# Strassen's products for gate and up in 12 pairs of column tiles, with adaLN columns by VectorE in the opening

## The chip, the cores and the metric

The kernel runs on one core of one Trainium2 chip. The metric is the device time of one execution in microseconds (us), taken as the median of several runs; lower is better. Engines are named as the profile names them: PE (TensorE), DVE (VectorE), ACT (ScalarE), POOL (GpSimd) and SP (SyncE, which issues most loads).

## The reference

One layer of a streaming encoder on 512 tokens of width 1024, all in float32. Each sub-layer gets shift, scale and gate from a conditioning vector c ("adaLN"):

```python
mod = (silu(c) @ w_ada + b_ada)            # 9 x 1024 numbers
h = rms_norm(x, g_pre) * (1 + scale) + shift
h = (silu(h @ w_gate) * (h @ w_up)) @ w_down     # FFN, D_FF = 2816
x = x + 0.5 * (1 + gate) * rms_norm(h, g_post)
... # mixer: spatial gating group and attention with forgetting, one projection in, one out
... # a second FFN like the first, with weights and adaLN numbers of its own
```

## The kernel before

All activations lie transposed: features on partitions (eight k-tiles of 128), the 512 tokens on the free axis. The order on every engine is written out by the program: code order is issue order (`manual_schedule`), and generators registered with `beside` put in their steps when `tick(us)` says that so many us of matmuls have gone by.

Precision comes from splitting. Each float32 operand is a high part (a cast by ACT) and a low part (float32 minus high, by DVE), and `mm3` makes each product of three matmuls, high x high, high x low, low x high. Weights are split on the chip: `Pair.hi` (L193) casts, `Pair.lo` (L203) subtracts; for some weights of the mixer `lo` runs as an ACT negation and an accumulating DMA from POOL's queue (L200, L201).

An FFN has 22 column tiles f of 128 gate and 128 up columns. `gate_up` runs 48 matmuls of 512 tokens for a tile (2 x 8 k-tiles x 3), `activate` turns the two results into the hidden tile h[f]: silu by ACT (L474), times up by DVE (L475), cast by ACT (L476), low part by DVE (L479). GROUPS splits the 22 tiles into 7, 7 and 8. After each group the eight output tiles m get the group's share (`pd`), copied into y by ACT for the first group (L542) and added by DVE for the others (L544). The last group does this in two halves of 256 tokens, so that the closing norm of one half runs beside the downs of the other. In the second FFN, the first four tiles also run in halves, since x arrives in halves.

Loads come through a queue of expected sources (`expect`, `load_next`) into the pool rp, two buffers of 1 MB. adaLN's columns are sums along rows of w_ada times silu(c): `mod_column` (L297) is one DVE instruction with an accumulated output. In the opening, a list of steps written by hand (START), the columns for k-tiles 0 and 1 are instead made by PE (BY_PE, matmuls into ps_mod, L306); the six others by DVE. The normalised x tile (xt, L647; high part of xm by ACT, L649; low part by DVE, L651) of a k-tile can be made when its columns are there, and the matmuls of the first three column tiles go k-tile by k-tile behind it. silu(c) as a row on all partitions (`crow`) is a broadcast DMA followed by an ACT silu. The other seven sets of columns come between the groups' steps (`between`).

Of the kernel before, what the change touches and what calls it, by code (L numbers as in the profile page):

```python
# [17 lines left out]
P = 128  # L18
D = 1024
# [6 lines left out]
GROUPS = (range(0, 7), range(7, 14), range(14, 22))  # L26
# [8 lines left out]
    1.3, 0, 0.9, 0.9, 0.7, 0.9, 0.8, 0, 0, 1.7, 1.9, 0, 0, 0.7, 1.4, 0.2, 1.6, 1, 0.5, 0.2, 0.6,  # L35
    0.7, 0, 1.1, 0.4, 0.4, 0, 0, 0.4, 1.6, 0.4, 0.7, 0.4, 1, 0.7,
# [3 lines left out]
    1.2, 1.4, 1.7, 1.7, 0, 9, 0.4, 0.4, 0, 0.7, 1.3, 0.7, 1.2, 0.7, 0.7, 0.7,  # L40
# [20 lines left out]
def pace(name, usual):  # L61
# [4 lines left out]
BY_PE = (0, 1)  # L66

# [22 lines left out]
def kernel(ctx: ExitStack, tc: tile.TileContext, a: dict, out: bass.AP):  # L90
# [81 lines left out]
    def expect(src, width):  # L172
        loads.append((src, width))
# [3 lines left out]
    def load_next(parts=1):  # L177
        if loads:
            src, width = loads.pop(0)
            raw = rp.tile([P, 2 * WSLOT], F32, tag="raw", name="raw")  # L180
            for i in range(parts):
                c = slice(i * width // parts, (i + 1) * width // parts)
                nc.sync.dma_start(raw[:, c], src[:, c])
            arrived.append(raw)

    class Pair:
        def __init__(self, n):
            self.n, self.raw, self.u, self.done = n, arrived.pop(0), [None, None], 0

        def hi(self, j, alloc=None):  # L190
            w = [P, 2, WSLOT] if alloc is None else [P, 2, D]
            self.u[j] = (alloc or wtile)(w, F32R, "wu")
            nc.scalar.copy(self.u[j][:, 0, : self.n], self.raw[:, j * self.n : (j + 1) * self.n])  # L193


        def lo(self, j, how="vector"):
            u, n = self.u[j], self.n
            raw, hi = self.raw[:, j * n : (j + 1) * n], u[:, 0, :n].bitcast(F32)
            if how == "transfer":
                nc.scalar.activation(u[:, 1, :n], hi, AF.Copy, scale=-1.0)  # L200
                nc.gpsimd.dma_start(u[:, 1, :n], raw, accum_op=ALU.add)  # L201
            else:
                (nc.vector if how == "vector" else nc.gpsimd).tensor_sub(u[:, 1, :n], raw, hi)  # L203
            self.done += 1
            if self.done == 2:
                load_next()
# [8 lines left out]
    def mm3(ps, lh, ll, rh, rl, start, stop):  # L215
        nc.tensor.matmul(ps, lhsT=lh, rhs=rh, start=start, stop=False)  # L216
        nc.tensor.matmul(ps, lhsT=lh, rhs=rl, start=False, stop=False)  # L217
        nc.tensor.matmul(ps, lhsT=ll, rhs=rh, start=False, stop=stop)  # L218
        return 3 * ps.shape[-1] * MM
# [75 lines left out]

    def mod_column(j, kt, raw):
        nc.vector.scalar_tensor_tensor(raw, raw, 1.0, crow, op0=ALU.mult, op1=ALU.mult,  # L297
                                       accum_out=msum[:, j * KT + kt : j * KT + kt + 1])

    def mod_first(kt, raws):  # L300
        both = lambda c: c[:, : 2 * KT].rearrange("p (j k) -> p j k", j=2)[:, :, kt]
        if kt in BY_PE:
            ps = psax("ps_mod")
            for j in range(2):
                for k in range(KT):
                    nc.tensor.matmul(ps[:, j : j + 1], lhsT=raws[j][:, k], rhs=sc[:, k : k + 1], start=j + k == 0, stop=j == 1 and k == KT - 1)  # L306
            src = ps[:, :2]
        else:
            for j in range(2):
                mod_column(j, kt, raws[j])  # L310
            src = both(msum)
# [1057 lines left out]
```

## Time and profile before

| what | value |
|---|---|
| median of 3 runs | 1037.07 us (1035.49 to 1040.47) |
| the profiled execution | 1040.04 us, of which the span 1038.2 |
| mean granted clock of PE | 0.974 |
| PE busy | 992.6 us, 5246 matmuls |
| DVE busy | 543.5 us, 1032 instructions |
| ACT busy | 398.5 us, 677 instructions |
| POOL busy | 66.5 us, 65 instructions |
| HBM read | 125.94 MB |

A line of a group reads: line of the kernel, engine, operation, output and input by name, shape, count | busy time in us, mean ns of one | idle time of the engine ahead of them and what ended it. A window reads: start and end in us, length, then for PE, weight loads, DVE, ACT and POOL the busy time with the count, the granted PE clock, the share of the DMA engines and GB/s. In a line of the timeline, the two first numbers are start and length, and the bracket holds the idle time ahead and what ended it. The stages in us: opening to 67.7, rest of the first FFN to about 410, mixer to about 652, second FFN to the end.

### The profile page before, as it was taken

To read this page: it belongs to the slowest core of one execution; us is meant where nothing else is said; L and a number is where in the kernel's file an instruction comes from. 1 tells how busy PE (TensorE), PEld (TensorE's weight loads), DVE (VectorE), ACT (ScalarE), POOL (GpSimd) and SP (SyncE) were. 2 spreads that over 40 slices of the span, in tenths; PEclk is the share of its full clock that TensorE was granted. 3 is DMA by queue.
4 is the path that set the end of the run, shared out by engine and by line. 5 is a ranking of instruction groups with operands and counts; after the bars stand their busy time and mean duration, and the time that the engine had idled before them with its cause. 6 is when DMAs were issued, how large, how long until landed. Compare 5 with 4: busy or idle time off the path is not lost.

```text
span 1038.2 us, 13121 instructions
## 1 busy us (share of the span) xinstructions
PE 992.6 (96%) x5246; PEld 839.2 (81%) x5246; DVE 543.5 (52%) x1032; ACT 398.5 (38%) x677; POOL 66.5 (6%) x65
## 2 busy tenths in 40 slices
PE   7999999999999998899999789999999999999994
PEld 5788888888888898788778679998888888888894
DVE  3885545456534458765766567863222333323345
ACT  5243232232223325543766657753232222223322
POOL 0000000000000002103203203100000000000011
PEclk9899999999999998999999779999999999999998
DMA  9745556446443333644424324633323223222102
GB/s 347 288 151 194 198 208 214 177 157 242 169 156 122 128 138 102 162 143 137 102 62 143 81 62 104 161 111 112 122 86 112 72 78 120 97 106 81 42 11 72
DMA packets 29773, 139.38 MB, mean 134 GB/s; under 512 B 3344, under 2 KB 5648, under 8 KB 21392
## 3 DMA queue, kind: packets, MB, share of 16 engines
q1 hardware_dynamic: 26832, 128.05, 34.4%
q0 software_dynamic: 2880, 10.50, 5.4%
q8 instruction: 41, 0.67, 0.3%
q14 instruction: 20, 0.16, 0.0%
HBM read 125.94 MB, written 2.10 MB: 123 GB/s over the span
## 4 chain that ended last, share of the span: by engine, by line
PE 43%; DVE 8%; ACT 5%; issue 2%; POOL 1%; DMA 1%; DVEq 0%; POOLq 0%; ACTq 0%
PE pd L218 4%; PE pd L217 4%; PE pd L216 4%; PE pg L218 4%; PE pg L217 4%; PE pu L218 4%; PE pu L217 4%; PE pu L216 4%; PE pg L216 4%; ACT p L966 1%; ACT wu L193 1%; DVE p L972 1%; PE pz L217 1%; PE pz L218 1%; DVE nmx L963 1%
## 5 line engine op out<-in xcount | busy, mean ns | idle before, releaser
L193 ACT CAST wu<-raw 128x1024 fp32r<-128x1024 f32 (+2 forms) x164 | 162.2, 1025 | 57.3 <-PE pd L218 53.3
L203 DVE TENSOR_TENSOR wu<-raw,wu 128x1024 fp32r<-128x1024 f32 (+2 forms) x132 | 151.6, 1188 | 58.3 <-ACT wu L193 57.3
L218 PE MATMUL pd<-h,wu 128*128 128x256 f32 (+1 forms) x480 | 161.2, 336 | 0.0
L216 PE MATMUL pd<-h,wu 128*128 128x256 f32 (+1 forms) x480 | 161.2, 336 | 0.0
L217 PE MATMUL pd<-h,wu 128*128 128x256 f32 (+1 forms) x480 | 160.7, 335 | 0.0
L475 DVE TENSOR_TENSOR sg<-sg,pu 128x512 f32<-128x512 f32 (+1 forms) x48 | 30.8, 642 | 230.1 <-PE pu L218 224.5
L216 PE MATMUL pg<-xm,wu 128*128 128x512 f32 (+1 forms) x360 | 135.1, 375 | 0.2 <-ACT sg L474 0.2
L218 PE MATMUL pu<-xm,wu 128*128 128x512 f32 (+1 forms) x360 | 135.1, 375 | 0.0
L217 PE MATMUL pg<-xm,wu 128*128 128x512 f32 (+1 forms) x360 | 134.4, 373 | 0.7 <-DVE xm L415 0.7
L218 PE MATMUL pg<-xm,wu 128*128 128x512 f32 (+1 forms) x360 | 134.8, 374 | 0.0
L217 PE MATMUL pu<-xm,wu 128*128 128x512 f32 (+1 forms) x360 | 134.0, 372 | 0.0
L216 PE MATMUL pu<-xm,wu 128*128 128x512 f32 (+1 forms) x360 | 133.6, 371 | 0.0
L476 ACT CAST h<-sg 128x512 fp32r<-128x512 f32 (+1 forms) x48 | 28.1, 586 | 219.7 <-DVE sg L475 219.7
L217 PEld LDWEIGHTS pd<-h,wu 128*128 128x128 f32 x480 | 91.4, 190 | 10.2
L218 PEld LDWEIGHTS pd<-h,wu 128*128 128x128 f32 x480 | 91.6, 191 | 9.8
L216 PEld LDWEIGHTS pd<-h,wu 128*128 128x128 f32 x480 | 91.4, 190 | 9.7
L217 PEld LDWEIGHTS pg<-xm,wu 128*128 128x128 f32 x360 | 67.8, 188 | 14.2 <-DVE xm L415 0.9
L217 PEld LDWEIGHTS pu<-xm,wu 128*128 128x128 f32 x360 | 67.6, 188 | 13.6
L218 PEld LDWEIGHTS pg<-xm,wu 128*128 128x128 f32 x360 | 67.6, 188 | 13.2
L216 PEld LDWEIGHTS pg<-xm,wu 128*128 128x128 f32 x360 | 67.6, 188 | 13.0 <-ACT sg L474 0.3
L216 PEld LDWEIGHTS pu<-xm,wu 128*128 128x128 f32 x360 | 67.7, 188 | 12.4
L218 PEld LDWEIGHTS pu<-xm,wu 128*128 128x128 f32 x360 | 67.6, 188 | 12.4
(226 smaller groups left out, 1468.4 us busy)
## 6 DMA issues: line engine op xcount, KB each, us to landing
raw<-wgu SPq DMA_DIRECT2D x43, 1024.0 KB, 4.7
mraw<-w_ada SPq DMA_DIRECT2D x49, 512.0 KB, 4.4
raw<-wd SPq DMA_DIRECT2D x16, 896.0 KB, 4.5
mrawh<-w_ada SPq DMA_DIRECT2D x19, 512.0 KB, 5.7
wu<-raw POOLq DMA_DIRECT2D x18, 512.0 KB, 5.0
raw<-wd SPq DMA_DIRECT2D x8, 1024.0 KB, 4.8
raw<-wz SPq DMA_DIRECT2D x4, 1024.0 KB, 6.5
raw<-wqk SPq DMA_DIRECT2D x4, 1024.0 KB, 4.9
```

The source lines that it names most:

```text
L193: nc.scalar.copy(self.u[j][:, 0, : self.n], self.raw[:, j * self.n : (j + 1) * self.n])
L203: (nc.vector if how == "vector" else nc.gpsimd).tensor_sub(u[:, 1, :n], raw, hi)
L216: nc.tensor.matmul(ps, lhsT=lh, rhs=rh, start=start, stop=False)
L217: nc.tensor.matmul(ps, lhsT=lh, rhs=rl, start=False, stop=False)
L218: nc.tensor.matmul(ps, lhsT=ll, rhs=rh, start=False, stop=stop)
L475: nc.vector.tensor_mul(sg, sg, pu[:, :n])
L476: nc.scalar.copy(h[f][:, 0, cs], sg)
L963: nc.vector.tensor_reduce(nmx, ps[:, :nk], axis=AX.X, op=ALU.max, negate=True)
L966: nc.scalar.activation(p[:, :nk], ps[:, :nk], AF.Exp, bias=nmx, accum_out=den)
L972: nc.vector.tensor_scalar(p[:, :nk], p[:, :nk], den, None, op0=ALU.mult)
```

## The change

*Pairs.* 12 pairs of neighbouring column tiles (4 pairs in the first FFN, f 12 to 19; 8 in the second, f 4 to 19) are computed by Strassen's scheme. The 2 x 2 blocks are: tokens in two halves, k in two halves, and the two column tiles of the pair. Seven products of blocks replace eight. A product is 24 matmuls of 256 tokens (gate and up, 4 k-tiles, 3 each). They run in the order 1, 2, 6, 5, 7, 3, 4, and some of the additions behind them are made by accumulation in PSUM: bank a receives products 1, 6, 7, 4 one onto the other, bank b product 2, bank c products 5 and 3. Between two accumulations into bank a, ACT copies what stands in it (m1, u2, u3 in `do_keep`). The other additions, silu, product, cast and low part are the steps of `do_out`, of 256 tokens each (the additions of 512, gate and up at once).

*Sums ahead of the products.* Products 6, 5, 7, 3 use sums S1 to S4 of x's blocks, made once per FFN by `sums_of_x` on DVE and ACT. Products 5, 6, 7, 4 use sums of weights, T1 to T4, made per pair: T1 and T3 by an ACT negation and an accumulating DMA of 512 KB from POOL's queue, T2 and T4 by a DVE subtraction (L864). Then high and low parts of each as before.

*Plan.* Groups are now 4, 4, 4, 4 and 6. A class Plan lists the blocks of matmuls of an FFN (product, plain, down) and puts every other step (take, hi, lo, sum, keep, out, down_out, ...) at a block number and an order within it; entries of the table PACE named b_... and o_... shift single steps. In a group with pairs, products of the next pair, plain tiles or early downs stand between the last products of a pair.

*Pools and loads.* rp has four buffers of half the size, hp four of twice the size; each load is half as large (512 KB), and the columns of adaLN but the last set are loaded into hp in the first FFN (`ada`). The last set comes in 16 halves in the second FFN. Pace and engine of other steps (low weights of the mixer among them) change through PACE.

*Opening.* All k-tiles' columns are made by DVE. `crow` is made by eight PE matmuls and two ACT copies, placed ahead of the squares of x.

```diff
-GROUPS = (range(0, 7), range(7, 14), range(14, 22))
+GROUPS = (range(0, 4), range(4, 8), range(8, 12), range(12, 16), range(16, 22))
+PAIRED = range(12, 20), range(4, 20)
...
-BY_PE = (0, 1)
...
+    "b_keepm1M1": 1, "b_keepu2M1": 1, "b_lo1F1": 0, "b_out21lowL1": 1, ...
...
-    hp_ = ctx.enter_context(tc.tile_pool(name="hp", bufs=8))
+    hp_ = ctx.enter_context(tc.tile_pool(name="hp", bufs=4))
-    rp = ctx.enter_context(tc.tile_pool(name="rp", bufs=2))
+    rp = ctx.enter_context(tc.tile_pool(name="rp", bufs=4))
...
-        elif op == "C":
-            nc.sync.dma_start(crow, rows_c.partition_broadcast(P))
-        elif op == "c":
-            nc.scalar.activation(crow, crow, AF.Silu)
+        elif op == "C":
+            for half, ps in enumerate((keep, psmm("ps_row"))):
+                for k in range(4):
+                    nc.tensor.matmul(ps[:, k * P : (k + 1) * P], lhsT=sc[:, 4 * half + k : 4 * half + k + 1].broadcast_to([P, P]), rhs=ident,
+                                     start=k == 0, stop=k == 3)
+                nc.scalar.copy(crow[:, half * T : (half + 1) * T], ps)
...
+    SUMS_LEAD = 34
+    def sums_of_x(us):
...
+                if ns[0] == 1:
+                    v = summed(add, a21, a22)
+                    yield us
+                    split(1, v)
+                    sub(v, v, a11[0])
...
+        def do_product(p, n):
+            b, fresh = {1: ("a", True), 2: ("b", True), 5: ("c", True), 6: ("a", False), 7: ("a", False), 3: ("c", False), 4: ("a", False)}[n]
+            if fresh:
+                bank[p, b] = ps_mm.tile([P, 2, HT], F32, tag="mm", name=f"bank_{b}")
+            ps, w = bank[p, b], W.pop((p, n))
...
+            for e in range(2):
+                for k in range(KT // 2):
+                    c = slice(k * P, (k + 1) * P)
+                    t = mm3(ps[:, e], w[:, e, 0, c], w[:, e, 1, c], moving(n, k, 0), moving(n, k, 1),
+                            fresh and e + k == 0, e == 1 and k == KT // 2 - 1, not fresh)
+                tick(4 * t)
...
+        def do_sum(p, t):
...
+            if t in (1, 3):
...
+                nc.scalar.activation(sums[p, n], both(raw(*key)), AF.Copy, scale=-1.0)
+                used_up(*key)
+                nc.gpsimd.dma_start(sums[p, n], both(a["wst"][s, p - PAIRED[1].start // 2, t // 2, 1]), accum_op=ALU.add)
+            else:
+                key = "wst", p, 1, 1 if t == 2 else 0
+                nc.vector.tensor_sub(sums[p, n], both(raw(*key)), sums[p, 5 if t == 2 else 6])
...
+        def do_keep(p, name):
...
+            q[p, name] = t2("q").rearrange("p (e t) -> p e t", e=2)
+            nc.scalar.copy(q[p, name], bank[p, "a"])
...
+        for b, (kind, *args) in enumerate(plan.blocks):
...
+            run_tasks(b)
...
+            does[kind](*args)
```

Three places show how the order moves. First PE, at the end of a group's downs (pd) in the first FFN, where the tiles that are paired now begin. Before, the plain gate matmuls of tile 14 (pg) follow:

```order
L218 MATMUL pd<-h_1477,wu 128x512
L216 MATMUL pd<-h_1547,wu 128x512
L217 MATMUL pd<-h_1547,wu 128x512
L218 MATMUL pd<-h_1547,wu 128x512
L216 MATMUL pg<-xm_195,wu 128x512
L217 MATMUL pg<-xm_195,wu 128x512
L218 MATMUL pg<-xm_195,wu 128x512
```

Now the first product of the pair (f 12, 13) follows, then the second with bank b (rows between them left out here), and the group's last down and the first product on a sum of x (S_1497) with summed weights (W_1764):

```order
L227 MATMUL pd<-h_1471,wu 128x512
L225 MATMUL bank_a<-xm_188,W_1660 128x256
L226 MATMUL bank_a<-xm_188,W_1660 128x256
L227 MATMUL bank_a<-xm_188,W_1660 128x256
```

```order
L227 MATMUL bank_a<-xm_279,W_1660 128x256
L225 MATMUL bank_b<-xm_342,W_1707 128x256
L226 MATMUL bank_b<-xm_342,W_1707 128x256
L227 MATMUL bank_b<-xm_342,W_1707 128x256
```

What moved is the whole gate and up work of these tiles, into matmuls of half the tokens that take turns between banks.

Second DVE, over the same downs. Before, low weights (wu), columns of adaLN (mraw) and additions into y:

```order
L544 TENSOR_TENSOR y_974<-y_974,pd 128x512 x2
L203 TENSOR_TENSOR wu<-raw,wu 128x1024 x2
L297 SCALAR_TENSOR_TENSOR mraw,msum<-mraw,crow 128x1024
L297 SCALAR_TENSOR_TENSOR mrawh,msum<-mrawh,crow 128x1024
L544 TENSOR_TENSOR y_1035<-y_1035,pd 128x512 x2
L203 TENSOR_TENSOR wu<-raw,wu 128x1024 x2
```

Now sums of x (sx and S), low parts for products 1, 2 and 6 (W), the weights' T sums and an addition of bank b, in this order:

```order
L846 TENSOR_TENSOR W_1707<-raw,W_1707 128x2x512
L917 TENSOR_TENSOR y_768<-y_768,pd 128x512
L864 TENSOR_TENSOR T_1671<-raw,T_1671 128x1024
L468 TENSOR_TENSOR S_1611<-sx,S_1611 128x2x256
L810 TENSOR_TENSOR wu<-raw,wu 128x512
L864 TENSOR_TENSOR T_1686<-raw,T_1671 128x1024
L472 TENSOR_TENSOR sx<-xm_417,S_1497 128x512
L473 TENSOR_TENSOR sx<-xm_417,S_1497 128x512
L474 TENSOR_TENSOR sx<-sx 128x512
L892 TENSOR_TENSOR q<-q,bank_b 128x512
L846 TENSOR_TENSOR W_1764<-T_1671,W_1764 128x2x512
```

The low part for product 6 (the last row) stands behind all of these.

Third DVE in the opening. Before, the row norm (r) comes first and the first columns (mod) come from PE:

```order
L611 SCALAR_TENSOR_TENSOR r_171<-r_171 128x512
L312 TENSOR_TENSOR mod<-ps_mod,cols 128x2
L330 SCALAR_TENSOR_TENSOR G_0_115<-mod,cols 128x1
L647 SCALAR_TENSOR_TENSOR xt_210<-x_94,G_0_115,r_171 128x512
L635 TENSOR_TENSOR wu<-raw,wu 128x1024
L651 SCALAR_TENSOR_TENSOR xm_195<-xt_210,mod,xm_195 128x512
```

Now:

```order
L301 SCALAR_TENSOR_TENSOR mraw_149,msum<-mraw_149,crow 128x1024 x2
L308 TENSOR_TENSOR mod<-msum,cols 128x2
L328 SCALAR_TENSOR_TENSOR G_0_117<-mod,cols 128x1
L1073 SCALAR_TENSOR_TENSOR r_189<-r_189 128x512
L1074 SCALAR_TENSOR_TENSOR r_189<-ps_stat,r_189 128x512
L1075 SCALAR_TENSOR_TENSOR r_189<-r_189 128x512
L1114 SCALAR_TENSOR_TENSOR xt_208<-x_96,G_0_117,r_189 128x512
L1100 TENSOR_TENSOR wu<-raw,wu 128x1024
L1118 SCALAR_TENSOR_TENSOR xm_188<-xt_208,mod,xm_188 128x512
```

The two column instructions of k-tile 0 moved onto DVE, ahead of the row norm, and the same holds for k-tile 1.

More of the change, by code (lines that the diff above doesn't have):

```diff
@@ L442, in ysl, with ffn @@
+    plans = [Plan(r) for r in PAIRED]
+    def ffn(s, i, begun, units, behind, hook, half_done):
+        h, ytile, plan = {}, {}, plans[s]
         def ysl(m, cs):
@@ new lines, in do_down @@
+        def do_down(g, m, half, fs, first, last):
+            cs = ALL if half is None else HALVES[half]
+            n = cs.stop - cs.start
+            if first:
+                dps[m] = psmm("pd")
+            ps, u, start = dps[m], du[g, m], GROUPS[g].start
+            after(("dlo", g, m))
+            if last:
+                done.add(("down", g, m, half))
+            for f in fs:
+                after(*([("h", f, c.start) for c in ((T1ST, T2ND) if half is None else (cs,))]))
+                c = slice((f - start) * P, (f - start + 1) * P)
+                w = mm3(ps[:, :n], u[:, 0, c], u[:, 1, c], h[f][:, 0, cs], h[f][:, 1, cs], first and f == fs[0], last and f == fs[-1])
+            if g < plan.last:
+                tick(len(fs) * w)
@@ new lines, in do_plain @@
+        def do_plain(f, e):
+            if e == 0:
+                psp[f] = psmm("pg"), psmm("pu")
+            u = gu.pop((f, e))
+            after(("plo", f, e))
+            done.add(("plain", f, e))
+            for k in range(KT):
+                c = slice(k * P, (k + 1) * P)
+                w = mm3(psp[f][e], u[:, 0, c], u[:, 1, c], xm[k][:, 0, :], xm[k][:, 1, :], k == 0, k == KT - 1)
+                if k % 4 == 3:
+                    tick(4 * w)
+        raws, sums, uses, q = {}, {}, {}, {}
@@ new lines, in do_activate, with both, do_hi @@
+        def do_activate(f):
+            after(("plain", f, 0), ("plain", f, 1))
+            activate(f, psp[f], ALL)
+            if i == 2 and f == NF - 1:
+                warm(AF.Abs_reciprocal_sqrt)
+        B = {1: (0, 0), 2: (1, 0), 3: (1, 1)}
+        def both(r):
+            return r[:, :D].rearrange("p (e n) -> p e n", e=2)
+        def do_hi(p, n):
+            if n not in B:
+                after(("sum", p, SUM[n]))
+            w = W[p, n] = wtile([P, 2, 2, T], F32R, f"W{n}")
+            nc.scalar.copy(w[:, :, 0, :], both(raw("wst", p, *B[n])) if n in B else sums[p, n])
@@ new lines, in ffn @@
+        if plan.paired:
+            first6 = next(b for b, w in enumerate(plan.blocks) if w[0] == "product" and w[2] == 6)
+            us = 0
+            begin_s = first6
+            while begin_s > 0 and us < SUMS_LEAD:
+                begin_s -= 1
+                us += plan.us(begin_s)
+        for b, (kind, *args) in enumerate(plan.blocks):
+            if begun and plan.paired and b == begin_s:
+                ensure(*FIRST_ADA)
+                s_gen = both_rounds(sums_of_x(2.6))
+                side_s = beside(s_gen)
+            run_tasks(b)
+            if not forms and kind == "product" and args[1] == 6:
+                finish_side(side_s)
+                for _ in s_gen:
+                    pass
+            does[kind](*args)
+            if kind == "down" and args[0] == plan.last:
+                tick(len(args[3]) * 3 * HT * MM)
@@ L677, in between, with ensure, flush @@
                 mod_finish(j)
-        while late and len(held) < 1 + spare:
-            held.append(mod_load_late(*late.pop(0), len(held) == 1))
+                have_mod.add(j)
+            if i:
+                ada_load()
+    def ensure(*js):
+        while not have_mod.issuperset(js):
+            ada()
+    for _ in range(3):
+        ada_load()
+    def flush(keep=0):
+        while len(held) > keep:
+            j, kt, half, raw = held.pop(0)
+            mod_column(j, kt, raw, crow[:, half * T : (half + 1) * T], (msum, msum2)[half])
+            if kt == KT - 1 and half:
+                mod_finish(j)
+                have_mod.add(j)
+    def between():
+        flush(room[0] - 1 if late else 0)
+        if late:
+            held.append(mod_load_late(*late.pop(0)))
     pv = [None] * 4
@@ L692, in mix_weights @@
             if step[0] == "h":
-                while spent[0] <= j:
+                while spent[0] < (j if j < 4 else KT):
                     yield pace("mix_weights0", 0.3)
```

690 lines of the change are left out of this document (499 added, 191 removed), and 35 rows, old and new, of the table PACE.

## The prediction, made before the changed kernel ran

> **What bounds the kernel now.** I read the page first: the share of each engine, the clock row and the chain of waits. Then windows by stage, to see where TensorE (PE) stands still; then lines by form, for the price of each kind of instruction; then the timeline of the opening and of the gap behind FFN1.
>
> ```profile
> PE 992.6 (96%) x5246; PEld 839.2 (81%) x5246; DVE 543.5 (52%) x1032; ACT 398.5 (38%) x677; POOL 66.5 (6%) x65
> PEclk9899999999999998999999779999999999999998
> PE 43%; DVE 8%; ACT 5%; issue 2%; POOL 1%; DMA 1%; DVEq 0%; POOLq 0%; ACTq 0%
> ```
>
> PE is busy for 96% of the span and leads the chain of waits, so matmul time taken out of a PE-bound stage comes off the end, as long as what feeds PE keeps up. Which stages are PE-bound, the windows say (columns: length; busy time and count of PE, weight loads, DVE, ACT, POOL; granted clock; DMA share; GB/s):
>
> ```profile
> 0.00:29.30 29.30, 21.54 (x121) 17.64 (x121) 11.33 (x20) 17.63 (x22) 0.20 (x4) 0.88 0.93 353
> 29.30:67.70 38.40, 35.91 (x147) 28.08 (x147) 32.53 (x57) 10.51 (x14) 0.00 (x0) 0.96 0.47 173
> 67.70:378.00 310.30, 310.30 (x1432) 255.85 (x1431) 159.48 (x227) 88.74 (x117) 0.74 (x1) 1.00 0.51 183
> 378.00:440.00 62.00, 54.05 (x361) 50.27 (x361) 48.27 (x118) 30.78 (x61) 13.05 (x12) 0.92 0.45 128
> 701.00:979.00 278.00, 278.00 (x1202) 225.41 (x1201) 89.13 (x97) 74.90 (x96) 0.00 (x0) 1.00 0.27 96
> 979.00:1004.00 25.00, 25.00 (x216) 25.00 (x216) 9.46 (x19) 11.40 (x21) 0.00 (x0) 1.00 0.01 2
> 1004.00:1038.20 34.20, 21.13 (x175) 20.50 (x173) 20.54 (x45) 8.26 (x18) 6.85 (x8) 0.86 0.19 62
> 402.10:410.10 8.00, 8.00 (x50) 8.00 (x50) 4.57 (x11) 2.15 (x5) 0.73 (x1) 0.67 0.90 297
> ...
> 689.47:700.69 11.22, 11.22 (x99) 11.22 (x98) 8.23 (x12) 7.75 (x12) 0.00 (x0) 1.00 0.48 159
> ```
>
> In the plain gate/up and down stages (67.70 to 378 and 701 to 979) PE never pauses, DVE works half and a third of the time. 278.00/1202 gives 0.2313 us per matmul of 512 columns. In 979 to 1004 PE does nothing but 256-column matmuls, each with its own weight load: 25.00/216 = 0.1157 us. The last row holds 96 whole gate/up matmuls of 256 columns (three more of its 99 reach in over its edges): 11.22/96 = 0.1169. I take the mean, 0.1163.
>
> **The change part by part.** *Products.* By the count of instructions in the two programs, 1152 gate/up matmuls of 512 columns go (24 column tiles times 48) and 2016 of 256 columns come (12 pairs, 7 products, 24 each). 1152 x 0.2313 = 266.5 us; 2016 x 0.1163 = 234.5 us. That is −32.0 us; with 0.1157 it is −33.2, and with 0.1169 −30.8. Both kinds lie on the path, since PE is the path there. Half the columns cost half the time in the row above, so the scheme's 7/8 arrives whole, if the products stream.
>
> [...]
>
> *Downs.* Five groups in place of three do the same products: 192 matmuls of 256 columns fewer (−22.3 us), 96 of 512 more (+22.2). Nothing. The additions into y rise from 16 to 48 of 512 columns on DVE and stand beside PE, as they do now.
>
> *Work for DVE and ACT inside a pair.* Their prices:
>
> ```profile
> L193 ACT CAST wu<-raw 128x1024 fp32r<-128x1024 f32 x128 | 129.6, 1046 | 57.3 <-PE pd L218 53.3 <-issue 3.6 <-DMA raw<-wgu 0.4
> L203 DVE TENSOR_TENSOR wu<-raw,wu 128x1024 fp32r<-128x1024 f32 x98 | 115.7, 1220 | 56.6 <-ACT wu L193 56.6
> L479 DVE TENSOR_TENSOR h<-sg,h 128x512 fp32r<-128x512 f32 x40 | 27.6, 690 | 16.5 <-ACT h L476 16.5
> L542 ACT COPY y<-pd 128x512 f32<-128x512 f32 x16 | 9.4, 588 | 52.1 <-PE pd L218 52.1
> L479 DVE TENSOR_TENSOR h<-sg,h 128x256 fp32r<-128x256 f32 x8 | 3.4, 425 | 3.8 <-ACT h L476 3.8
> L475 DVE TENSOR_TENSOR sg<-sg,pu 128x256 f32<-128x256 f32 x8 | 3.3, 416 | 5.5 <-ACT sg L474 5.5
> L476 ACT CAST h<-sg 128x256 fp32r<-128x256 f32 x8 | 3.2, 406 | 8.8 <-DVE sg L475 8.8
> L474 ACT ACTIVATE sg<-pg 128x256 f32<-128x256 f32 x8 | 3.0, 377 | 5.2 <-PE pg L218 5.2
> ```
>
> A pair gives DVE nine passes over 1024 elements (seven low parts, two T sums), three additions of 512 and eight steps of 256 for h: 9 x 1.18 (L203's 1220 ns less the overlap of neighbours, an estimate) + 3 x 0.69 + 4 x 0.416 + 4 x 0.425 = 16.1 us. ACT: 9 x 1.046 + 3 x 0.588 + 4 x 0.377 + 4 x 0.406 = 14.3 us. PE has 168 x 0.1163 = 19.5 us. So PE stays the bound with 17% and 27% to spare and the work costs nothing by itself; the cover is PE's own stream, and if it went, each pair would last DVE's 16.1 us at least. But DVE and ACT take their work in order. Behind a DVE step that waits for a cast stand the next low weights, which PE waits for. Bounds from the rows: 0, or L203's present idle of 56.6/98 = 0.58 us at each of the nine low steps, which makes 16.1 + 5.2 = 21.3, 1.8 us over PE in each pair. Today's DVE can afford that idling, so I stand near the lower end, with +2 us for all 12 pairs.
>
> *Copies of bank a.* Product 6 adds to what product 1 left in the bank, 7 to 6, 4 to 7; ahead of each an ACT copy (0.588) must have read the bank. One other product, 24 x 0.1163 = 2.8 us, lies between, so the copy is hidden unless ACT is over two casts late. Nothing; the loss is a rival.
>
> *T sums by POOL's queue.* 24 accumulating DMAs of 512 KB.
>
> ```profile
> wu<-raw POOLq DMA_DIRECT2D x18, 512.0 KB, 5.0
> ```
>
> Such a DMA took 5.0 us to land. Plan sets it some six blocks (16 us) ahead of the product, so it is hidden. A pair moves 2 MB of weights and 1 MB of these in 19.5 us, 154 GB/s, below the 183 of the PE-bound window above. Nothing.
>
> *Entry into pairs, FFN1.* Here the sums of x, low down weights, additions into y and the first T sums meet on DVE. From the activation of column tile 10 to the low part for product 6 the new order has 49 passes of 512 and 6 of 1024: 49 x 0.69 + 6 x 1.22 = 41.1 us. PE has one plain tile and the downs of a group, 144 x 0.2313, and products 1 and 2, 48 x 0.1163: 38.9 us. That is 2.2 us late without any waiting. Eight of the sums wait for their ACT cast; L479's idle per instruction now, 16.5/40 = 0.41, adds 3.3. I take +5.5, between 0 (if some of the passes come earlier than I see) and 9.
>
> *Entry, FFN2.* The low part of the second down weights stands behind eight passes of the sums, 5.6 us, while PE holds one down of 2.6. One gap of +3, 0 to 8.
>
> *Clock after such gaps.* Between FFN1 and mixer the trace has one gap:
>
> ```profile
> 401.20 1.22 PE L367 MATMUL ps_stat<-k,cr 128*128 128x128 f32 x4 [2.73 <-DVE cr L233]
> ```
>
> In the 8 us behind it (row 402.10, granted clock 0.67) 50 matmuls took 0.16 us each in place of 0.1163: 2.2 us lost. Two new gaps of about this size, part of them short of it: +3 (0 to 5). [...]
>
> *Opening.* Columns of adaLN for k-tiles 0 and 1 move from PE to DVE.
>
> ```profile
> 21.40 1.06 ACT L639 ACTIVATE crow<-crow 128x1024 f32<-128x1024 f32 x1
> 25.14 0.16 DVE L312 TENSOR_TENSOR mod<-ps_mod,cols 128x2 f32<-128x2 f32 x1 [3.79 <-PE ps_mod L306]
> 30.94 1.22 DVE L297 SCALAR_TENSOR_TENSOR mraw<-mraw,crow 128x1024 f32<-128x1024 f32 x1
> 35.95 1.22 DVE L297 SCALAR_TENSOR_TENSOR mraw<-mraw,crow 128x1024 f32<-128x1024 f32 x1
> 57.40 1.22 DVE L297 SCALAR_TENSOR_TENSOR mraw<-mraw,crow 128x1024 f32<-128x1024 f32 x1
> 61.74 0.75 DVE L651 SCALAR_TENSOR_TENSOR xm<-xt,mod,xm 128x512 fp32r<-128x512 f32 x1 [0.79 <-ACT xm L649]
> ```
>
> DVE spends 5.0 us per k-tile (30.94 to 35.95), starts on its first at 30.94 and ends the sixth at 62.5; the gate matmuls follow it. After the change k-tile 1 is its own as well. Its weights are there between 21.3 and 25.1 (it waited 3.79 for PE until 25.14), so seven tiles end 6 x 5.0 + 5.1 later, at 56.4 to 60.2, a gain of 2.3 to 6.1. The crow copies, of the order of 1.06 us, now stand on ACT ahead of the squares of x and can take 1.1 back. I take −3 (−1 to −5). SP's loads are the same bytes in halves, less crow's 512 KB.
>
> *Ends of the FFNs.* The last group has 6 tiles instead of 8, so a half's downs last 144 x 0.1163 = 16.7 us instead of 22.3 and cover less of the closing norm of the other half. In the windows 378 to 440 and 1004 to 1038 PE pauses 8 and 13 us. The pauses can grow by up to 2 each, while other steps are retimed: 0 (−3 to +4).
>
> *Sum* against the profiled execution (1040.04; span 1038.2): −32 − 3 + 2 + 5.5 + 3 + 3 + 0 = −21.5, so 1018.5. The median of the runs is 1037.07, 3.0 lower than that execution, so 1015.5; I say 1015.
>
> **Rivals.** All times as medians.
> (a) The entries fit. DVE runs 41.1 us against 38.9 only if nothing was done earlier; then −32 − 3 remain with a little loss: 1002 to 1006. For it: DVE is half idle in the stage before. Against: the order puts sums behind the adaLN passes.
> (b) DVE's in-order queue becomes the bound inside pairs. If every low step keeps today's 0.58 us, 1.8 x 12 = 21.6 us are given back: 1015 + 20 = about 1035; if half the pairs do, 1025. It decides from 0.38 us of waiting per low step (19.5 − 16.1, over nine). For it: L203's idle row; against: that idling is DVE with nothing else to do.
> (c) Slower. ACT's copy of bank a stands behind three 1.046 casts and a 0.377 activation: 3.5 + 0.588 less 2.8 of cover is 1.3 us, 36 times = 47: 1037 − 35 + 47 = 1049. It decides from (35 + 5)/36 = 1.1 us per copy. Against: ACT has 27% to spare.
> (d) The loads of the products' weights don't hide.
>
> ```profile
> L218 PEld LDWEIGHTS pd<-h,wu 128*128 128x128 f32 x480 | 91.6, 191 | 9.8
> ```
>
> A load lasts 191 ns; paid in line, 2016 x 0.191 = 385 us come on top: about 1400. The 25.00 us for 216 of each kind exclude it as far as a trace can. [...]
>
> **How the numbers follow.** The likeliest, small slips at the entries (1007 to 1022), has 0.50; (a) 0.20; (b) 0.22, of which a fifth lands within half a per cent of 1037; (c) 0.07; (d) 0.01. About 0.5% (5 us) is what a measurement of this kernel can tell from no change. Faster: 0.50 + 0.20 + 0.18 = 0.88; same 0.05; slower 0.07. The range leaves out (c), (d) and the upper part of (b): 1001 to 1030.
>
> **What would show it.** Products: a window inside FFN2 with only 256-column matmuls at about 0.1163 each, clock 1.00 and no PE idle. Entry of FFN1: a PE gap of some 2 to 6 us before the first matmul of bank a on a sum of x, released by DVE's low part, and a clock below 1 behind it. Entry of FFN2: a gap at a down, released by DVE. Opening: the last xm low part at about 57 to 60. (b) would show as many short PE gaps released by DVE's W in every pair, (c) as gaps released by ACT's q. The prediction is wrong if those gaps exceed 15 us in sum, or if the 256-column matmuls run at more than 0.12.

## The result, and the profile after

The changed kernel is slower: median 1054.4 us (1051.9 to 1054.94, 4 runs) against 1038.77 us before (1035.49 to 1041.76, 4 runs), a ratio of 1.0144 with the interval [1.0118, 1.0170]. The forecast was 1015. The profiled execution took 1051.9 us, its span 1050.1. Two single runs that lie far from all others (2391.51 us of the mixer's numbers, 3286.81 us of the weights off the power of two) are left out of the medians below.

The head of the page of the changed kernel:

```profile
PE 976.8 (93%) x6000; PEld 860.5 (82%) x6000; DVE 710.6 (68%) x1326; ACT 489.7 (47%) x864; POOL 104.1 (10%) x96
PEclk8999999999999998999899979999999999999998
PE 65%; DVE 17%; DMA 7%; ACT 6%; issue 4%; POOL 2%; DVEq 0%; SPq 0%; ACTq 0%; POOLq 0%
```

PE's busy time fell by 16 us and the span grew by 12, so PE now stands idle 28 us longer. Where, the windows by stage tell. First the changed kernel, then the kernel before; the edges are the first plain gate tile, the first matmul of the mixer (pvf) and the first gate matmul of the second FFN:

```profile
0.00:67.06 67.06, 54.89 (x244) 42.12 (x245) 48.56 (x85) 25.70 (x34) 0.20 (x4) 0.90 0.77 282
67.06:410.00 342.94, 331.99 (x1884) 287.83 (x1882) 242.90 (x387) 139.85 (x218) 16.74 (x20) 0.99 0.52 172
410.00:665.52 255.52, 228.40 (x1370) 195.42 (x1371) 168.31 (x445) 134.53 (x302) 60.83 (x43) 0.93 0.35 99
665.52:1050.10 384.58, 361.48 (x2506) 335.10 (x2504) 250.84 (x411) 189.66 (x312) 26.34 (x30) 0.97 0.42 117
```

```profile
0.00:67.69 67.69, 57.43 (x265) 45.70 (x266) 43.85 (x76) 28.12 (x36) 0.20 (x4) 0.92 0.67 251
67.69:410.18 342.49, 338.85 (x1643) 283.74 (x1642) 184.67 (x286) 101.91 (x143) 7.84 (x8) 0.99 0.50 177
410.18:652.13 241.95, 224.47 (x1361) 191.94 (x1360) 161.49 (x431) 144.67 (x311) 48.30 (x41) 0.94 0.39 109
652.13:1038.20 386.07, 371.86 (x1984) 317.85 (x1982) 153.47 (x242) 123.80 (x189) 10.19 (x12) 0.99 0.28 92
```

By lengths, after less before: opening −0.6, first FFN +0.5, mixer +13.6, second FFN −1.5. Two things stand out. The mixer, in which the change has no products, lost most. And both FFNs, which have the products, gained next to nothing. PE's waits of the changed kernel (who waited, for whom; us in total, times, longest; most of the rows left out lie in the opening or at the mixer's two ends):

```profile
PE pd L227 <- DVE wu L810: 10.2, 10, 3.2
...
PE pz L226 <- DMA wu<-raw: 4.9, 1, 4.9
...
PE pgt L225 <- ACT vh L1364: 2.5, 1, 2.5
PE pd L225 <- ACT wu L806: 1.9, 1, 1.9
...
PE bank_a L227 <- DVE W L846: 1.4, 2, 0.8
...
PE psc L1405 <- DVE lf L1401: 1.1, 1, 1.1
```

The products (bank_a) hardly wait. The downs do, for the low parts of their weights; so do, in the mixer, z (for its weights), the gating matmuls (pgt, for the normalised v) and the sums of log-forget (psc). The products themselves are a little slower than forecast; a window over exactly seven of them:

```profile
754.91:774.99 20.08, 20.08 (x169) 20.08 (x168) 13.62 (x18) 13.12 (x19) 1.73 (x2) 1.00 0.51 126
```

20.08/168 = 0.1195 us per matmul, 2.87 per product.

### The profile page after: what moved, and what is told of

The parts are those of the page before. It is cut to its first block, busy times and chain, and to the rows that moved or that the text cites. A ratio compares the mean times of both kernels' runs of the same rounds, so it can differ in the third digit from the quotient of the medians.

```text
span 1050.1 us, 15422 instructions
## 1 busy us (share of the span) xinstructions
PE 976.8 (93%) x6000; PEld 860.5 (82%) x6000; DVE 710.6 (68%) x1326; ACT 489.7 (47%) x864; POOL 104.1 (10%) x96
## 4 chain that ended last, share of the span: by engine, by line
PE 65%; DVE 17%; DMA 7%; ACT 6%; issue 4%; POOL 2%; DVEq 0%; SPq 0%; ACTq 0%; POOLq 0%
PE pd L227 5%; PE pd L225 5%; PE pd L226 5%; PE bank_a L227 4%; PE bank_a L225 4%; PE bank_a L226 4%; PE pu L227 3%; PE pu L225 3%; PE pu L226 3%; PE pg L227 3%; PE pg L225 3%; PE pg L226 3%; DMA raw<-wst 2%; PE bank_c L225 2%; PE bank_c L227 2%
## 5 line engine op out<-in xcount | busy, mean ns | idle before, releaser
L227 PE MATMUL pd<-h,wu 128*128 128x512 f32 (+1 forms) x448 | 158.4, 354 | 10.4 <-DVE wu L810 10.2
L225 PE MATMUL pd<-h,wu 128*128 128x512 f32 (+1 forms) x448 | 157.4, 351 | 1.9 <-ACT wu L806 1.9
L226 PE MATMUL pd<-h,wu 128*128 128x512 f32 (+1 forms) x448 | 156.3, 349 | 0.0
L226 PEld LDWEIGHTS pd<-h,wu 128*128 128x128 f32 x448 | 85.6, 191 | 10.8
L301 DVE SCALAR_TENSOR_TENSOR mraw<-mraw,crow 128x1024 f32<-128x1024 f32 (+1 forms) x80 | 87.3, 1117 | 2.5 <-DMA mraw<-w_ada 2.5
L806 ACT CAST wu<-raw 128x512 fp32r<-128x512 f32 (+1 forms) x80 | 51.3, 660 | 43.6 <-PE pd L227 20.4
L810 DVE TENSOR_TENSOR wu<-raw,wu 128x512 fp32r<-128x512 f32 (+1 forms) x80 | 58.2, 739 | 10.0 <-ACT wu L806 9.8
L227 PE MATMUL pu<-xm,wu 128*128 128x512 f32 (+1 forms) x168 | 59.5, 354 | 1.0 <-DMA wu<-raw 1.0
L225 PE MATMUL pu<-xm,wu 128*128 128x512 f32 (+1 forms) x168 | 59.6, 354 | 0.0
L226 PE MATMUL pu<-xm,wu 128*128 128x512 f32 (+1 forms) x168 | 59.4, 353 | 0.0
L227 PE MATMUL pg<-xm,wu 128*128 128x512 f32 (+1 forms) x168 | 58.9, 351 | 0.3 <-DVE wu L819 0.3
L225 PE MATMUL pg<-xm,wu 128*128 128x512 f32 (+1 forms) x168 | 59.1, 352 | 0.0
L226 PE MATMUL pg<-xm,wu 128*128 128x512 f32 (+1 forms) x168 | 58.8, 350 | 0.0
L846 DVE TENSOR_TENSOR W<-T,W 128x1024 fp32r<-128x1024 f32 x48 | 58.4, 1218 | 0.0
L227 PE MATMUL bank_a<-S,W 128*128 128x256 f32 x192 | 54.6, 284 | 1.5 <-DVE W L846 1.4
L225 PE MATMUL bank_c<-S,W 128*128 128x256 f32 x192 | 54.6, 284 | 0.2
L227 PE MATMUL bank_a<-xm,W 128*128 128x256 f32 x192 | 54.3, 283 | 0.0
```

Of the source, the lines that this page charges most:

```text
L301: nc.vector.scalar_tensor_tensor(raw, raw, 1.0, c, op0=ALU.mult, op1=ALU.mult, accum_out=to[:, j * KT + kt : j * KT + kt + 1])
L806: nc.scalar.copy(du[g, m][:, 0, :n], raw("wd", g, m)[:, :n])
L810: nc.vector.tensor_sub(u[:, 1, :n], raw("wd", g, m)[:, :n], u[:, 0, :n].bitcast(F32))
L846: nc.vector.tensor_sub(w[:, :, 1, :], src, w[:, :, 0, :].bitcast(F32))
```

## The experiments

Theory: the pairs do save matmul time, but the change also moved three supplies into places where PE waits: low down weights behind other work on DVE's queue, a column of adaLN in front of the mixer's statistics, and the mixer's weights behind a shorter last group. The rival is that the pairs themselves cost what they save. The kernel before ran beside each group of experiments; times from different groups are compared through their ratios to it. Lengths of stages come from one profiled execution each and are good to some 2 us: the mixer took 249.1 to 251.4 us in the six runs with pairs in both FFNs that share the early half columns (below).

**No pairs.**

```diff
-PAIRED = range(12, 20), range(4, 20)
+PAIRED = range(12, 12), range(4, 4)
```

> All 22 column tiles of both FFNs run plain (no Strassen pairs, no sums of x); the groups 4, 4, 4, 4, 6, the opening, the pools and the mixer stay as in the changed kernel (median 1054.4). Theory A (the pairs do gain, and what ate the gain lies mostly elsewhere, in the mixer): the products' 26 us come back on, the waits at the entries into pairs (about 16 us with the clock behind them) mostly go, so 1060 to 1066, with the mixer still near 255 us. Rival B (the pairs gain nothing, their waits cost what they save): 1050 to 1056. Rival C (the pairs cost more than they save): under 1050.

Measured: 1057.48 us, ratio 1.0190 [1.0157, 1.0222]. The pairs are worth 3 us in the changed kernel by the medians and 5 by the ratios, and the intervals overlap; the time lies between A and B and settles neither. One thing is settled: everything else in the change costs about 20 us. In the trace without pairs the first FFN ends at 410.2, as with them; the second takes 387.9 against 384.6.

**The mixer's numbers.** The 53 pacing numbers and engine choices, and both FILL lists, as in the kernel before.

> The changed kernel with the kernel before's values for all pacing numbers and engine choices that are not those of the pairs' plan (53 entries of PACE, and the two FILL lists). Theory A (the mixer's extra 13 us come from these retimed numbers): 1042 to 1047. Rival B (they come from what the change had to do to the pools: big tiles in hp, half loads in rp, z weights that wait for the last down, half columns of adaLN in the mixer): 1052 to 1057 or slower, and the gaps ahead of psc and pgt stay.

Measured: 1055.61 us, ratio 1.0173 [1.0117, 1.0229]: by the whole time rival B; giving the numbers back does not mend the kernel. The first FFN and the mixer together got 1.6 us shorter, the second FFN 5.4 longer. But this does not clear the numbers of a part in the mixer's loss: the mixer alone took 249.2 us in place of 255.5, and the first FFN 347.6 in place of 342.9 with a wait of 4.3 us for the closing norm ahead of the mixer's first matmul. The wait of pgt stays at 2.1 us.

**Half columns used up earlier.** What delays the mixer is seen on DVE, in the timeline of the changed kernel, between the last z tile and the row statistics (L233, which begin the normalisation of v and are followed by log-forget):

```profile
495.30 0.69 DVE L301 SCALAR_TENSOR_TENSOR mraw<-mraw,crow 128x512 f32<-128x512 f32 x1 [2.10 <-DMA mraw<-w_ada]
495.92 0.08 DVE L301 DVE_READ_ACCUMULATOR mraw<-mraw,crow 128x1 f32 x1
495.92 0.17 DVE L233 TENSOR_SCALAR rs<-ag 128x2 f32<-128x2 f32 x1
```

DVE waits 2.10 us for a half column of adaLN that nobody needs before the second FFN, and behind it stand the statistics. On PE, in the timeline:

```profile
501.49 0.75 PE L1405 MATMUL psc<-tri,lf 128*16 128x512 f32 x4 [1.12 <-DVE lf L1401]
505.54 0.58 PE L225 MATMUL pgt<-vh,wsh 128*128 128x256 f32 x1 [2.54 <-ACT vh L1364]
```

The last two calls in the z loop only use up what is held:

```diff
-        between()
+        between() if tt < 2 else flush()
```

> The changed kernel, but the last two of the four calls in the loop over z tiles that load a half column of adaLN do not load; they only use up what is held (the loads follow in the second FFN). Theory A (VectorE's wait for the last half column, 2.1 us, and the column passes ahead of it hold up the row statistics behind it in order, and with them log-forget and the spatial norm): the waits of psc (1.1 us) and pgt (2.5 us) shrink to under 1 together, the clock there stays near 1.00, time 1047 to 1050. Rival B (the POOL and ScalarE chain behind it is what is late): 1053 to 1055.

Measured: 1046.15 us, ratio 1.0080 [1.0047, 1.0112]: theory A, and more than it asked. Both waits are gone but for 0.34 us, the statistics begin at 492.79, and the clock is 1.00 over the 22 us of the second window. Windows over this place, first the changed kernel from its first wait on, then this run:

```profile
501.00:505.00 4.00, 1.51 (x7) 0.79 (x7) 4.00 (x4) 1.42 (x3) 3.76 (x3) 1.00 0.08 20
505.00:509.00 4.00, 3.31 (x14) 2.79 (x14) 3.80 (x10) 3.68 (x5) 1.53 (x1) 0.52 0.29 111
509.00:512.00 3.00, 3.00 (x16) 2.77 (x17) 1.25 (x5) 0.46 (x2) 0.85 (x1) 0.51 0.37 132
```

```profile
485.00:507.00 22.00, 21.63 (x109) 17.29 (x108) 19.20 (x41) 11.52 (x18) 14.50 (x10) 1.00 0.08 28
```

The mixer takes 249.2 us instead of 255.5. The two waits were 3.7 us together. Behind them the granted clock stood at 0.52 and 0.51 for 7 us, which is worth another 3.4 (7 x 0.48, an estimate): by this estimate about half of the loss was the waits and half the clock.

**The opening without some dummy matmuls.**

```diff
-    ... u1.0 h1.1 v1.1 W2 g0.1 u0.1 G1.0 g1.0 k16 G1.1 ... U1.1 k10 u1.1 ...
+    ... u1.0 h1.1 v1.1 W2 g0.1 u0.1 G1.0 g1.0 G1.1 ... U1.1 u1.1 ...
```

> The changed kernel without 16 and 10 of the dummy matmuls that the opening puts between gate and up matmuls (the first 12 stay). They take 4.0 and 2.4 us of TensorE, in a stretch that has no idle time behind 38.9 us. Theory A (TensorE is the bound of the new opening, the dummies and a low clock stand in its way): the first plain tile starts 3 to 6 us earlier than at 67.1, time 1048 to 1052. Rival B (they only fill time in which TensorE would wait for x, and hold the clock up): 1053 to 1057, the clock before 40 us lower.

Measured: 1053.89 us, ratio 1.0154 [1.0120, 1.0187]: rival B in its first half; the time that the dummies filled became waits for xm. Those waits in this run, and in the changed kernel:

```profile
PE pg L1126 <- ACT xm L1116: 8.3, 4, 3.5
```

```profile
PE pg L1126 <- ACT xm L1116: 5.4, 2, 3.0
```

The mean clock from 20 to 40 us was 0.74 in both, so B's second half, a lower clock without the dummies, isn't seen. DVE's chain of k-tiles still sets the end of the opening; its rows in the changed kernel, the first column of k-tile 1, of k-tile 2, and the last low part of xm:

```profile
22.83 1.22 DVE L301 SCALAR_TENSOR_TENSOR mraw<-mraw,crow 128x1024 f32<-128x1024 f32 x1
...
31.13 1.22 DVE L301 SCALAR_TENSOR_TENSOR mraw<-mraw,crow 128x1024 f32<-128x1024 f32 x1
...
62.01 0.75 DVE L1118 SCALAR_TENSOR_TENSOR xm<-xt,mod,xm 128x512 fp32r<-128x512 f32 x1 [0.79 <-ACT xm L1116]
```

**Low down weights first, second FFN.** DVE and PE at the first downs of the second FFN in the changed kernel: sums of x (S, sx) run ahead of the low part of the second down weights (L810), for which PE waits. And ACT 26 us later waits for the load of a down weight, which SP issued at 738.73. It stands in SP's queue behind loads whose buffers such low parts gave back, the last of them ending at 737.98; it then took 9.6 us to land, so that the low parts are only a part of this wait:

```profile
718.15 0.69 DVE L468 TENSOR_TENSOR S<-sx,S 128x512 fp32r<-128x512 f32 x1
...
720.98 0.69 DVE L468 TENSOR_TENSOR S<-sx,S 128x512 fp32r<-128x512 f32 x1 [0.68 <-ACT S L467]
721.59 0.69 DVE L810 TENSOR_TENSOR wu<-raw,wu 128x512 fp32r<-128x512 f32 x1
```

```profile
722.33 0.50 PE L227 MATMUL pd<-h,wu 128*128 128x512 f32 x1 [3.15 <-DVE wu L810]
```

```profile
748.45 0.62 ACT L806 CAST wu<-raw 128x512 fp32r<-128x512 f32 x1 [7.30 <-DMA raw<-wd]
```

On top of the early half columns, the first group's low parts one block earlier:

```diff
+    "b_down_lo01": -1, "o_down_lo01": 3.5,
```

> The early use-up of adaLN's half columns (that run measured 1046.2) and, in the second FFN, the low part of the first group's down weights one block earlier, ahead of the sums of x on VectorE. Theory A (the low down weights queue behind the sums, and the loads behind them, so TensorE loses about 10 us there with the clock): the waits of 3.2 us at the second down and of 1.9 and 1.1 at the held-back down go or shrink to under 2 in sum, time 1038 to 1043. Rival B (VectorE has too much to do in that stretch whatever the order; the wait moves to product 6): 1044 to 1047, a gap at the first matmul on a sum of x.

Measured: 1041.27 us, ratio 1.0016 [0.9996, 1.0035]: theory A. The second FFN fell from 382.4 to 378.2 us. The longest of PE's waits for low down weights, 3.2 us, is gone:

```profile
PE pd L227 <- DVE wu L810: 6.7, 10, 1.9
```

At the later down a wait of 1.1 us for ACT's cast stayed, and one of 1.2 us at the first product on a sum came up behind it, a small piece of what B said.

**A last group of eight, without pairs.**

```diff
-GROUPS = (range(0, 4), range(4, 8), range(8, 12), range(12, 16), range(16, 22))
+GROUPS = (range(0, 4), range(4, 8), range(8, 14), range(14, 22))
```

> No pairs (that run measured 1057.5), and groups of 4, 4, 6 and 8 column tiles in place of 4, 4, 4, 4 and 6: the last group's half has 192 matmuls again, 22 us instead of 17. Theory A (the shorter last half covers less of the closing norm and of the splitting of the mixer's first weights, so that the z weights load later and TensorE waits 5 to 6 us for them): the wait of pz falls to about 3 us, the stretch from the first pvf to the first gate of the second FFN from 257 to about 252, time 1050 to 1054. Rival B (those weights are late because of the half-size load buffers and the order of their split): pz still waits 5 us or more, 1055 to 1059.

Measured: 1051.46 us, ratio 1.0107 [1.0066, 1.0147], 6 us by the medians under the run with groups of 4 and 6 (9 by the ratios): theory A. The other groups differ too (4, 4, 6 in place of 4, 4, 4, 4), so the last group's part isn't separated from theirs by the time. The row of SP's timeline shows the loads of the first z weights (start, time over which four were issued), in the run without pairs and groups of 4 and 6, and in this run:

```profile
404.44 11.66 SPq L193 DMA_DIRECT2D raw<-wz  x4
```

```profile
399.46 10.89 SPq L193 DMA_DIRECT2D raw<-wz  x4
```

They start 5 us earlier, and the wait of pz, 6.1 us without pairs before, is gone; in its place stands one of 3.3 us for the closing norm's sum of squares from POOL. With pairs a last group of eight wasn't run.

**High and low parts off the power of two.**

```diff
-            w = W[p, n] = wtile([P, 2, 2, T], F32R, f"W{n}")
+            w = W[p, n] = wtile([P, 2, 2, T + 8], F32R, f"W{n}")[:, :, :, :T]
...
-            du[g, m] = (htile if g == plan.last and 4 <= m < KT - 1 else wtile)([P, 2, D], F32R, "wu")
+            du[g, m] = (htile if g == plan.last and 4 <= m < KT - 1 else wtile)([P, 2, n + 16], F32R, "wu")
```

> As the run with the low down weights first, but the low parts of the products' weights lie 2080 bytes behind the high parts instead of 2048, and those of the down weights 64 bytes further than the tile's width instead of 4096. Theory A (the 256-column matmuls go slower, 0.119 us against 0.117 in the kernel before, because high and low weights lie a power of two apart): 24 matmuls of a product take 2.80 to 2.82 us instead of 2.87, time 4 to 6 us below that run. Rival B (the rate has another cause): 2.87 as before, time within 1.5 us of that run.

Measured: 1040.19 us, ratio 1.0001 [0.9981, 1.0020]; by time it cannot be told from the run before it, rival B. The trace shows a small part of A, over the same seven products:

```profile
744.97:764.85 19.88, 19.88 (x170) 19.88 (x168) 15.21 (x19) 14.13 (x21) 1.73 (x2) 1.00 0.56 145
```

2.84 us per product instead of 2.87. It isn't this window alone: the products' matmuls start on average 0.1181 us apart in this run's second FFN and 0.1180 to 0.1182 in the three later runs with pairs and the spaced weights, against 0.1193 in the changed kernel and 0.1194 in the next run, which has them unspaced. What else makes these matmuls slower than 0.1169 stays open.

**All low down weights first.** On top of the early half columns, in place of the two numbers above:

```diff
-                    self.at(b - early + 1, 3, "down_lo", g, m)
+                    self.at(b - early, 6.5, "down_lo", g, m)
```

> The early use-up of adaLN's half columns, and the low parts of all down weights of all groups in both FFNs one block earlier, right behind their cast. Theory A (what the downs wait for is VectorE's order: adaLN columns, additions and sums stand ahead of low parts): the sum of TensorE's waits for low down weights falls from 10.8 us to under 4, time 1034 to 1041. Rival B (VectorE then waits for the cast itself and is late with other work: sums of x, products' weights): 1042 to 1048, with waits at the products instead.

Measured: 1038.34 us, ratio 0.9993 [0.9971, 1.0014]: theory A, with some of B:

```profile
PE bank_a L227 <- DVE W L846: 6.2, 4, 2.4
...
PE pd L227 <- DVE wu L810: 2.6, 3, 1.8
```

The downs' waits fell from 10.8 us to 2.6, the products' rose to 6.2. The first FFN ended at 406.8 instead of 411.0; the second, at 379.7 us, did a little worse than with only its first group moved.

**The mended kernel.** The early half columns, the low down weights first in the whole first FFN and in the first group of the second, the spaced weights.

> The changed kernel with the early use-up of adaLN's half columns, the low down weights one block earlier in the whole first FFN and in the first group of the second, and the weights' low parts off the power of two. Theory A (the parts add up: first FFN as in the run with all low parts early, 4 us shorter; second FFN as in the run with the first group's early, 378 us): 1033 to 1038, 1 to 5 us under the kernel before. Rival B (they eat the same slack, and VectorE is late elsewhere): 1038 to 1042.

Measured: 1033.71 us, ratio 0.9956 [0.9936, 0.9976]: theory A; it beats both kernels, the one before by about half a per cent. The first FFN ends at 405.7, the mixer takes 249.4 us, the second FFN 375.6.

**The mixer's weights split one by one.**

```diff
-"h0 h1 h2 h3 l0 l1 l2 l3 h4 h5 l4 l5 h6 h7 l6 l7"
+"h0 l0 h1 l1 h2 l2 h3 l3 h4 h5 l4 l5 h6 h7 l6 l7"
```

> As the mended kernel, and the mixer's first four weights are split high, low, high, low in place of four highs and then four lows, so that their load buffers come free one by one for the z weights. Theory A (the z weights are late because these four buffers are held until the low parts): TensorE's wait for pz falls from 5 to under 3 us, time 2 to 4 us below the mended kernel. Rival B (the low parts wait for the closing norm's work on VectorE and ScalarE anyway, or delay that norm): within 1.5 us, or slower by a longer wait ahead of pvf.

Measured: 1033.69 us, ratio 0.9952 [0.9931, 0.9973]: rival B. The wait stays:

```profile
PE pz L226 <- DMA wu<-raw: 4.4, 1, 4.4
```

**Pairs in the second FFN alone, and none, in the mended kernel.**

```diff
-PAIRED = range(12, 20), range(4, 20)
+PAIRED = range(12, 12), range(4, 20)
```

```diff
-PAIRED = range(12, 20), range(4, 20)
+PAIRED = range(12, 12), range(4, 4)
```

> As the mended kernel, but with no pairs in the first FFN. Theory A (pairs are worth about 25/12 = 2.1 us each before their waits; with 2 to 3 us lost at the entry into the first FFN's four pairs, these are worth some 4 to 6 us): 1037 to 1043, that is 3 to 6 us above the mended kernel. Rival B (the first FFN's pairs lose at their entry what they save): within 1.5 us of the mended kernel.

> As the mended kernel, but with no pairs at all. Theory A (without the mending the pairs were worth 3 us, since their waits gave back some 20 of 25; the mending removes about 10 of those waits): 1044 to 1050, 10 to 14 us above the mended kernel. Rival B (the mending helped the plain tiles as much): 3 to 5 us above the mended kernel.

Measured: 1038.67 us, ratio 1.0011 [0.9990, 1.0032], and 1050.14 us, ratio 1.0118 [1.0085, 1.0152]. The first is theory A; the second lies 16 us above the mended kernel, more than the 10 to 14 of theory A, and excludes its rival. Once their supplies are in order, the four pairs of the first FFN are worth 5 us and all twelve 16. Up to 3 of these 16 may not be the pairs' own, as the mending did nothing for the plain second FFN: it took 391.0 us here and 387.9 in the first run without pairs. And the 16 count from a kernel with all the rest of the change, which without pairs is still 11.6 us slower than the kernel before; against that one the pairs leave a gain of 4.8.

## Why the prediction was wrong, step by step

The forecast was −21.5 us and the profiled spans went +11.9: 33 us apart. Four terms make that up. The mixer and the opening are read from the windows and the products from theirs; the entries get what is left, by difference.

*Ends of the FFNs, "while other steps are retimed: 0 (−3 to +4)": the step that failed most.* The mixer lost 13.6 us. I looked for the change in what it adds to the FFNs and gave the stage between them one term, from the windows of pauses that it had before. I had seen that the last group covers less and that adaLN's last set comes in halves, and did not follow what is queued behind either. DVE's wait for a half column delayed the mixer's statistics, and the shorter cover made the z weights late. Where in the mixer the time went, the windows of its stretches tell: from its first matmul to the last of z, on to the last of the gating, and from the last matmul of pqk to the second FFN, first the kernel before, then the changed one:

```profile
410.18:484.90 74.72, 70.42 (x390) 60.88 (x388) 49.28 (x118) 35.47 (x68) 13.02 (x11) 0.98 0.50 152
484.90:501.26 16.36, 16.22 (x87) 13.16 (x86) 12.57 (x39) 12.12 (x17) 7.96 (x7) 1.00 0.19 40
...
557.92:652.13 94.21, 82.76 (x575) 74.16 (x574) 61.83 (x165) 61.05 (x136) 21.84 (x19) 0.87 0.37 96
```

```profile
410.00:489.51 79.51, 73.75 (x393) 63.92 (x394) 47.91 (x123) 32.81 (x65) 17.81 (x13) 0.94 0.51 149
489.51:512.68 23.17, 19.36 (x88) 15.50 (x86) 16.52 (x43) 10.67 (x17) 9.37 (x7) 0.85 0.16 57
...
567.28:665.52 98.24, 80.68 (x580) 72.33 (x579) 67.14 (x174) 57.37 (x134) 26.04 (x20) 0.91 0.34 92
```

That is +4.8, +6.8 and +4.0 us; what lies between got 2.1 shorter. The 6.8 is the half column: the run that removes it takes 16.9 us for that stretch. The 4.8 holds z's wait for its weights, 4.9 us against 2.7 before, and a new one of 1.8 us for x at the mixer's first matmul; with a last group of eight, without pairs, the stretch took 75.9 us against 79.8. The 4.0 at the end I had not looked for. There the run with the kernel before's numbers took 95.6 us, and all other runs of this record but the kernel before took 98 or more, so the retimed numbers have a part in it; no run separates which.

*Entries, steady slips and clock: +13.5 forecast, about 25 by difference.* What stands between the products' saving (26) and the FFNs' net (1) was given back. 16 of it is time in which PE stands idle: length less busy time in the windows by stage grew by 7.3 us in the first FFN and 8.9 in the second. The place and mechanism of the entry into the second FFN were right, a wait for DVE behind the sums, 3.15 against +3. But I counted one gap. A later down waited for ACT (1.92) and DVE (1.13) again, behind late low parts and a slow load, so that the entry's waits were 6.2 us. PE's rows at these places in the changed kernel's timeline, four of the first FFN and two of the second:

```profile
161.13 0.50 PE L227 MATMUL pd<-h,wu 128*128 128x512 f32 x1 [1.16 <-DVE wu L810]
...
219.19 0.50 PE L227 MATMUL pd<-h,wu 128*128 128x512 f32 x1 [1.19 <-DVE wu L810]
...
231.99 0.76 PE L227 MATMUL pd<-h,wu 128*128 128x512 f32 x1 [1.87 <-DVE wu L810]
...
248.30 0.39 PE L227 MATMUL bank_a<-S,W 128*128 128x256 f32 x1 [0.63 <-DVE W L846]
...
749.12 0.50 PE L225 MATMUL pd<-h,wu 128*128 128x512 f32 x1 [1.92 <-ACT wu L806]
750.97 0.79 PE L227 MATMUL pd<-h,wu 128*128 128x512 f32 x1 [1.13 <-DVE wu L810]
```

In the first FFN the entry came out near its forecast, but at another instruction. From 219 to 249 us PE waited 4.1 us against +5.5: only 0.63 of it ahead of the first product on a sum, the rest at the downs before it, whose low parts stand behind sums of x and additions on DVE (ahead of the one at 231.25, sums from 227.53 and three additions from 229.46). The wait at 161.13 is a slip that I had no term for: a group of four has 12 matmuls, 2.78 us, per down (I had written 2.6), and there two additions and a column of adaLN of 1.22 us stand ahead of the low part. I had costed regrouping the downs at nothing, naming DVE's additions as beside PE, without asking what is in line ahead of the low part that the next down needs. The rest of the 25, some 9 us against +3 for the clock, is slower matmuls. A part of it is the clock, as behind the waits of 1.87 us (0.79 over 8 us) and 3.15 us (0.83 over 10); behind the one of 1.16 it was 1.00 over 8 us:

```profile
161.00:169.00 8.00, 7.87 (x34) 6.46 (x35) 7.36 (x12) 1.05 (x1) 0.00 (x0) 1.00 0.84 286
232.00:240.00 8.00, 8.00 (x33) 6.68 (x34) 6.65 (x10) 1.12 (x2) 0.00 (x0) 0.79 1.00 253
722.33:732.33 10.00, 10.00 (x36) 8.02 (x37) 8.82 (x14) 1.76 (x3) 0.00 (x0) 0.83 0.53 159
```

*Products: −32.0 forecast, −26 measured.* 2016 x 0.1195 = 240.9 against 1152 x 0.2317 = 266.9. The mechanism was right and the size off by a fifth: 0.1195 us per matmul in place of 0.1163. A part of that is my reading. A window's count holds the records that reach in over its edges: in 979 to 1004 two of the 216 were such, so the true value there was 25.00/214 = 0.1168. In 701 to 979 it is two of 1202 as well, which makes 278.00/1200 = 0.2317, and in 402.10 to 410.10 three of 50 (0.17 us each, not 0.16).

*Opening: −3 forecast, −0.6 measured.* I took 5.0 us per k-tile for k-tile 1 too. It took 8.3 (22.83 to 31.13), since two low parts of the first weights and a wait of 1.72 us for their cast stand among its steps; two more made k-tile 3 longer, 6.5. (k-tile 1's columns run on DVE now, but behind the row norm, not ahead of it like those of k-tile 0.) The last low part of xm ended as late as before (62.01 and 61.74 at their start).

The rivals: (c), slower, came true in sign but not by its mechanism; among PE's waits none is for a copy of bank a. (b) did not occur: products wait 1.4 us in all. (d) was excluded rightly: in the window over seven products 168 weight loads and the matmuls take the same 20.08 us. (a) was the opposite of what happened. None of them looked outside the FFNs. Without the mixer's 13.6 us the time would have been about 1041, still above the range's 1030, so the terms inside the FFNs were too small by themselves. The signs named beforehand did not fire either: the gaps at the two entries sum to 10 us, not 15, and the products ran at 0.1195, not above 0.12. The chance of 0.07 for slower priced one mechanism where several independent ones led the same way.

## What to carry to other kernels

When a change also regroups and retimes, take the stages without the new work as seriously as those with it: list what each engine's queue holds ahead of the instruction that the bound engine waits for, and what buffer that instruction releases. A step that nobody needs soon (a sum, or a half column like the one for which DVE waited 2.10 us here) must not stand ahead of one that is needed at once; moving such steps, with the weights spaced, brought 20 us here and turned a loss of 1.4% into a gain of 0.4%. The worth of a saving depends on its supplies: twelve pairs were worth 3 to 5 us in the changed kernel and 16 in the mended one.

## What the runs showed of the hardware

Short waits cost more than their length in one place. Behind waits of 1.12 and 2.54 us, 4 us apart, the granted clock in the changed kernel was 0.52 and 0.51 for 7 us; the run without the half columns ahead of the statistics had all but 0.34 us of the waits gone and the clock at 1.00, and its mixer was 6.3 us shorter. Behind a wait of 1.87 us the clock was 0.79 over 8 us. Not every wait was followed by this: behind one of 1.16 us it was 1.00 over 8 us. What makes the difference, these runs do not show. Second, 256-column matmuls are not at one rate: 0.1169 us in the halves before, 0.1195 in the products, and 2.84 instead of 2.87 us per product in the run whose products' low weights lie 2080 bytes behind the high ones instead of 2048.
